# One modulation vector of the second layer is computed in the first FFN instead of at the end of the first mixing

## Chip, cores and metric

The kernel runs on one core of one Trainium2 chip. The metric is the device time of one execution in microseconds. Before the change the median of three runs is 1867.49 us (1861.09, 1867.49 and 1871.28).

## What is computed

Two layers of a diffusion backbone, over 256 context and 256 latent tokens of width 1024, in float32. Cut to what matters here:

```python
for l in range(DEPTH):                     # DEPTH = 2
    sh1, sc1, g1, sh2, sc2, g2 = jnp.split((s_lat @ mod_w[l] + mod_b[l])[:, None, :], 6, axis=-1)
    csh1, csc1, cg1, csh2, csc2, cg2 = jnp.split(s_ctx @ mod_w[l] + mod_b[l], 6, axis=-1)
    ... = _split(modulate(x, sh1, sc1) @ w_in[l], IN_SPLITS)
    ...
    o_l = gated_merge(gt_l, att_l @ w_o_attn[l],
                      short_conv(ch_l, cb_l, cc_l, conv_w[l]) @ w_o_conv[l],
                      rwo_l @ w_o_rwkv[l]) @ w_out[l]
    x_new = layer_norm(alpha * x + g1 * o_l, ln1_g[l], ln1_b[l])
    x_new = layer_norm(alpha * x_new + g2 * swiglu(modulate(x_new, sh2, sc2), ffn_w13[l], ffn_w2[l]),
                       ln2_g[l], ln2_b[l])
```

Each layer has six modulation vectors per stream: shift, scale and gate of the mixing (numbers 0, 1, 2) and of the FFN (3, 4, 5). They depend on the conditioning alone, not on the tokens, so they can be computed at any time before they are used. The pair (l, i) names vector i of layer l; both streams are computed together. (1, 0) is the shift of the second layer's mixing. It is first read at the end of the first layer's FFN, where the second norm's output is modulated for the second layer.

## The kernel before

All 512 tokens go through a layer together. A layer has two parts. The first is the mixing: the input projection in output blocks of 128 (features of the recurrent branch, compressed attention inputs, conv inputs, gates), the chunked scans of the recurrent branch, the attention, and three merges that add the branches, each through its output weights `wo` (function `merge`). Then the output projection, and the second part, the FFN: a loop over 22 turns `m` (line 865), each with two weight tiles of 1024x128 (gate and up, 48 matmuls in all), then a loop over 22 rows of the second weight.

Float32 products are made from three matmuls of split operands: each weight tile is loaded to `raw`, cast by ScalarE to `hi` (line 193), and VectorE or GpSimd makes `lo`, the remainder (line 194). `mm3` (lines 237 to 240) does the three matmuls. `raw` is a ring of three buffers (line 179), and `hi` and `lo` have four halves each.

The modulation vectors are computed in steps. One step (`mod`, line 253) loads 512 KB of `modw` into the same ring of `raw` buffers and does eight small matmuls (line 259). Every second step ends with a copy (line 265), a pick matmul (line 266) and an addition (line 291). A vector is eight steps. After a gate vector (2 or 5) one more step transposes it and stores it by rows (`mod_rows`, line 276).

The table `MODS` says which vectors are made in which list: for each layer, one list for the mixing and one for the FFN. In the first mixing a step follows each of the 24 gate blocks (line 614) and two steps stand in each of the four conv blocks (line 601); `mod_step(100)` on line 619 takes whatever is left of the list. In the first FFN two steps follow the first norm (line 852), one stands in each turn `m` of the loop while `m < N_FFN` (line 885), and line 934 takes the rest at the end.

In the first FFN the kernel also prepares 35 weight tiles of the second layer ahead of time (`ahead_list`, line 217): load `wraw`, cast `whi` on ScalarE (line 230), remainder `wlo` on GpSimd (line 231), and store both (lines 233 and 234).

The order of the program is not the order of the code alone: a scheduler places the instructions of each engine by its own estimate of time and respects data and buffers. All loads and stores named here are issued by SyncE, in order. `brs` are the loaded tiles of a branch, cast to `br` (line 642); `gts` are gate tiles and share three buffers with `brs`.

Of the kernel before, what the change touches and what calls it, by code (L numbers as in the profile page):

```python
# [51 lines left out]
N_CONV = (2, 1)  # L52
BC = 4
X_AT = 0
N_FFN = 10
N_LN1 = (2, 7)
LATE_AT = (2, 4, 6, 8)

# [1 line left out]
CP = 6  # L60
CONV_AT = (20, 4)
WO_EARLY = (2, 0)
MODS = ((((0, 2), (0, 3), (0, 4), (0, 5), (1, 0)), ((1, 1), (1, 2))), (((1, 3), (1, 4)), ((1, 5),)))
FLUSH = (30, 30)
DV = 0
UB = 1
# [10 lines left out]
def body(ctx: ExitStack, tc: tile.TileContext, A: dict, out: bass.AP, dbg=None, upto=None):  # L77
# [203 lines left out]
    def mod_list(todo, bank=None):  # L281
        for l, i in todo:
            for k0 in range(0, 8, MG):
                ps = []
                for j in range(MG):
                    def f(l=l, i=i, k0=k0, j=j, ps=ps):
                        if j == 0:
                            ps.append((bank or pg)())
                        mod(ps[0], l, i, k0 + j, j)
                        if j == MG - 1:  # L290
                            dve.tensor_tensor(out=modT[l][:, i, k0:k0 + MG], in0=mod_out(ps[0], MG),
                                              in1=mod_bias(l, i, k0, MG), op=ALU.add)
                    yield f
            if i in (2, 5):
                yield lambda l=l, i=i: mod_rows(l, i, bank)
# [152 lines left out]
    def layer(l, xh=None, xl=None, pre=()):  # L448
# [6 lines left out]
        share[0] = SHARE[l][0]  # L455
        mods = mod_list(MODS[l][0])

        def mod_step(n=1):
            for _ in range(n):
                f = next(mods, None)  # L460
                if f:
                    f()
# [344 lines left out]
        with ff, tc.tile_pool(name=f"ff{l}", reuse_waits="tile", bufs=1) as fp, banks(f"psf{l}"):  # L807
# [40 lines left out]

            mods = mod_list(MODS[l][1], pg if l else pf)
            one = post(l, 0, accs, fp, x2_out, res1, lambda tt: res_d[0 if l == 0 else 2][tt])  # L850
# [14 lines left out]
            for m in range(KF):  # L865
# [18 lines left out]
                hh.append(hl)  # L884
                if m < N_FFN:
                    mod_step()
# [510 lines left out]
```

## Time and profile before

| | |
|---|---|
| median of three runs | 1867.49 us |
| profiled execution | 1872.44 us |
| its span, first to last instruction | 1870.6 us |
| mean granted TensorE clock | 0.975 |
| TensorE matmuls busy | 1787.7 us, 96% |
| VectorE, ScalarE, GpSimd busy | 58%, 45%, 29% |
| DMA | 379.40 MB, 203 GB/s over the span |

The profile comes from one execution. The granted clock is TensorE's, as a share of its full 2.4 GHz; it has two levels, 2.4 and 1.2 GHz, and a figure between is a mean over a stretch. Busy time of TensorE counts a matmul until its modelled end. In the views an instruction is named by its engine, its line, its output and inputs by the program's names, and "<-" in brackets says what ended the idle time ahead of it. A float32 matmul (the modulation step, a transpose) is counted as two.

### The profile page before, as it was taken

The page shows a single profiled execution, that of the slowest core. Times are in us where ns is not written, and L with a number is a line of the kernel's source. Part 1 is how long each engine was busy: PE and PEld are TensorE (multiplying, and loading weights), DVE is VectorE, ACT ScalarE, POOL GpSimd, SP SyncE. Part 2 cuts the span into 40 slices and gives each one's busy share as a digit, 9 for nine tenths or more (in the row PEclk, how much of TensorE's full clock was granted, in tenths as well). Part 3 has the DMA queues.
Part 4 walks back from the last instruction along what each step waited for, and adds up shares of the span by engine and source line. Part 5 has one row for each costly group of instructions (what it writes and reads, how often), then busy time and mean ns, then how long its engine had stood idle before and what let it go on. Part 6 is the DMA issues. An engine that isn't in the chain of part 4 may idle for free.

```text
span 1870.6 us, 35371 instructions
## 1 busy us (share of the span) xinstructions
PE 1787.7 (96%) x13556; PEld 1469.7 (79%) x13556; DVE 1091.3 (58%) x2012; ACT 842.6 (45%) x1830; POOL 534.2 (29%) x550
## 2 busy tenths in 40 slices
PE   7999999999989999999999999999999999979997
PEld 5777877777768767877888887888788886869986
DVE  4457723873367777643444336168874468866655
ACT  2567333823245442444444313386524364535552
POOL 1466113611134221454343003344311132320001
PEclk9998999999989999999999999998899999989999
DMA  9443544343494326699999424775586673686563
GB/s 341 136 144 108 164 135 158 105 151 124 161 315 158 127 64 235 224 370 350 344 349 348 161 92 156 233 238 171 182 273 221 215 227 112 192 288 223 182 225 110
DMA packets 182410, 379.40 MB, mean 203 GB/s; under 512 B 33952, under 2 KB 89312, under 8 KB 182240
## 3 DMA queue, kind: packets, MB, share of 16 engines
q1 hardware_dynamic: 179264, 368.54, 58.8%
q10 hardware_dynamic: 2976, 8.59, 1.3%
q8 instruction: 107, 1.75, 0.4%
q14 instruction: 63, 0.52, 0.1%
HBM read 301.53 MB, written 75.53 MB: 202 GB/s over the span
## 4 chain that ended last, share of the span: by engine, by line
PE 71%; DMA 10%; DVE 9%; ACT 5%; issue 3%; SPq 1%; POOL 1%; ACTq 0%; POOLq 0%; DVEq 0%
PE pg L238 10%; PE pg L239 10%; PE pg L240 9%; PE p_f L238 9%; PE p_f L240 8%; PE p_f L239 8%; DMA raw<-in_win_dram 3%; PE p_G L1069 2%; PE p_G L755 2%; DVE lo L194 1%; DMA raw<-in_modw_dram 1%; ACT hi L193 1%; PE p_y L776 1%; PE pg L259 1%; DMA raw<-in_w_dram 1%
## 5 line engine op out<-in xcount | busy, mean ns | idle before, releaser
L194 DVE TENSOR_TENSOR lo<-raw,hi 128x512 fp32r<-128x512 f32 (+1 forms) x408 | 321.9, 799 | 352.5 <-ACT hi L193 348.9
L193 ACT CAST hi<-raw 128x512 fp32r<-128x512 f32 x478 | 286.9, 615 | 430.9 <-DMA raw<-in_win_dram 95.1
L238 PE MATMUL pg<-xh,hi 128*128 128x512 f32 (+1 forms) x912 | 331.6, 365 | 8.7 <-ACT gt L585 3.8
L240 PE MATMUL pg<-xh,lo 128*128 128x512 f32 (+1 forms) x912 | 327.0, 359 | 0.7 <-DMA lo<-win 0.6
L239 PE MATMUL pg<-xl,hi 128*128 128x512 f32 (+1 forms) x912 | 326.1, 358 | 0.4 <-DVE xl L246 0.4
L238 PE MATMUL p_f<-x2h,hi 128*128 128x256 f32 (+1 forms) x688 | 232.7, 338 | 4.6 <-ACT hi L193 4.6
L240 PE MATMUL p_f<-x2h,lo 128*128 128x256 f32 (+1 forms) x688 | 231.7, 337 | 0.9 <-DVE lo L194 0.5
L239 PE MATMUL p_f<-x2l,hi 128*128 128x256 f32 (+1 forms) x688 | 231.3, 336 | 0.0
L238 PEld LDWEIGHTS pg<-xh,hi 128*128 128x128 f32 x912 | 177.8, 196 | 40.1 <-issue 9.0
L240 PEld LDWEIGHTS pg<-xh,lo 128*128 128x128 f32 x912 | 178.8, 196 | 26.2 <-issue 3.0
L239 PEld LDWEIGHTS pg<-xl,hi 128*128 128x128 f32 x912 | 178.4, 196 | 22.6 <-issue 1.3
L194 POOL TENSOR_TENSOR lo<-raw,hi 128x512 fp32r<-128x512 f32 x70 | 92.0, 1314 | 342.8 <-ACT hi L193 279.1
L238 PEld LDWEIGHTS p_f<-x2h,hi 128*128 128x128 f32 x688 | 131.4, 191 | 19.7 <-ACT hi L193 6.5
L240 PEld LDWEIGHTS p_f<-x2h,lo 128*128 128x128 f32 x688 | 131.3, 191 | 15.3 <-DVE lo L194 2.1
L239 PEld LDWEIGHTS p_f<-x2l,hi 128*128 128x128 f32 x688 | 131.4, 191 | 12.8
L231 POOL TENSOR_TENSOR wlo<-wraw,whi 128x512 fp32r<-128x512 f32 x70 | 93.5, 1357 | 125.0 <-ACT whi L230 125.0
L334 POOL TENSOR_TENSOR rs<-rs,mhalf 128x1 f32<-128x1 f32 x12 | 8.8, 733 | 359.3 <-DVE rs L353 359.3
L1053 POOL TENSOR_TENSOR FM<-ta,di 64x256 f32<-64x256 f32 x64 | 56.0, 876 | 48.0 <-ACT FM L1047 17.3
L661 POOL TENSOR_TENSOR acc<-acc,gts 128x512 f32<-128x512 f32 (+1 forms) x32 | 38.4, 1209 | 80.0 <-DVE gts L659 61.9
L259 PE MATMUL pg<-raw,cs 128*32 128x128 f32 x1024 | 53.1, 303 | 6.0 <-DMA raw<-in_modw_dram 5.3
L1109 DVE TENSOR_TENSOR sq<-sq,iv 128x31 f32<-128x31 f32 (+15 forms) x124 | 49.2, 397 | 3.2
L483 POOL TENSOR_TENSOR nb<-pp 128x512 f32<-128x512 f32 (+1 forms) x30 | 30.4, 1012 | 71.8 <-ACT pp L480 60.5
(393 smaller groups left out, 3604.3 us busy)
## 6 DMA issues: line engine op xcount, KB each, us to landing
raw<-in_modw_dram SPq DMA_DIRECT2D x96, 512.0 KB, 4.8
raw<-in_w_dram SPq DMA_DIRECT2D x88, 512.0 KB, 5.1
raw<-in_win_dram SPq DMA_DIRECT2D x79, 512.0 KB, 4.4
raw<-in_ffn_w_dram SPq DMA_DIRECT2D x44, 512.0 KB, 3.8
wraw<-in_win_dram SPq DMA_DIRECT2D x35, 512.0 KB, 6.7
win<-whi SPq DMA_DIRECT2D x35, 512.0 KB, 6.0
win<-wlo SPq DMA_DIRECT2D x35, 512.0 KB, 5.4
hi<-win SPq DMA_DIRECT2D x70, 256.0 KB, 3.8
```

The costliest lines, as they stand in the source:

```text
L193: act.copy(out=hi, in_=r)
L194: e.tensor_tensor(out=lo, in0=r, in1=hi.bitcast(F32), op=ALU.subtract)
L231: pool.tensor_tensor(out=lo[:, s], in0=raw[:, s], in1=hi[:, s].bitcast(F32), op=ALU.subtract)
L238: pe.matmul(ps, wh, xh, start=first, stop=False, skip_group_check=True)
L239: pe.matmul(ps, wh, xl, start=False, stop=False, skip_group_check=True)
L240: pe.matmul(ps, wl, xh, start=False, stop=last, skip_group_check=True)
L259: pe.matmul(ps[32 * (k % 4):32 * (k % 4) + 32, 0:128], cs[:, o:o + 32], raw[:, k], start=(j == 0 and k < 4), stop=(k >= 4), skip_group_che ...
L661: pool.tensor_tensor(out=a, in0=a, in1=g, op=ALU.add)
L755: pe.matmul(ps[:, 0:nk], qT[:, h, qt * 128:(qt + 1) * 128], kT[:, h, 0:nk], start=True, stop=True)
L1053: pool.tensor_tensor(out=FM[r, :, k0:k0 + 64], in0=rc(ta[r]), in1=rc(Pi[r]), op=ALU.mult)
L1069: pe.matmul(ps[:, j * 128:j * 128 + ncol], FM[r, j], AR[z][r, e, hp, j, 0:ncol], start=True, stop=True)
L1109: dve.tensor_tensor(out=Ti[:, j + 1:32, 0:w], in0=Ti[:, j + 1:32, 0:w], in1=tv, op=ALU.subtract)
```

## The change

Vector (1, 0) moves from the end of the first mixing's list to the head of the first FFN's list. The steps in the loop of the FFN are allowed in 18 turns instead of 10. The code of the functions is the same.

```diff
-N_FFN = 10
+N_FFN = 18
...
-MODS = ((((0, 2), (0, 3), (0, 4), (0, 5), (1, 0)), ((1, 1), (1, 2))), (((1, 3), (1, 4)), ((1, 5),)))
+MODS = ((((0, 2), (0, 3), (0, 4), (0, 5)), ((1, 0), (1, 1), (1, 2))), (((1, 3), (1, 4)), ((1, 5),)))
```

The first mixing's list goes from 42 steps to 34, of which 32 are taken beside the gates and conv blocks. The first FFN's list goes from 17 steps to 25: 2 after the norm, 10 or 18 in the loop, and 5 at the end either way.

The first place is TensorE at the end of the first mixing, between the transpose of the first layer's last gate vector (line 276) and the merge of the conv branch. `br` numbers are the branch's tiles, `pg` the output blocks. Before:

```order
L276 MATMUL pg<-ident,modT_81 16x128
L259 MATMUL pg<-raw,cs 32x128 x24
L266 MATMUL pg<-pick,modrow 128x4
L259 MATMUL pg<-raw,cs 32x128 x16
L266 MATMUL pg<-pick,modrow 128x4
L1251 MATMUL p_y<-ident,gn 128x128 x4
L259 MATMUL pg<-raw,cs 32x128 x8
L1236 MATMUL p_y<-ident,Yf 128x128 x4
L1270 MATMUL p_G<-sg,lw 128x256
...
L1270 MATMUL p_G<-sg,lw 128x256
L259 MATMUL pg<-raw,cs 32x128 x8
L238 MATMUL pg<-br,hi 128x512
```

With the change:

```order
L276 MATMUL pg_5688<-ident_69,modT0_81 16x128
L238 MATMUL pg_5800<-br_5770,hi_5790 128x512
L238 MATMUL pg_5816<-br_5770,hi_5790 128x512
L238 MATMUL pg_5842<-br_5770,hi_5832 128x512
L239 MATMUL pg_5800<-br_5770,hi_5790 128x512
L240 MATMUL pg_5800<-br_5770,lo_5791 128x512
L238 MATMUL pg_5800<-br_5775,hi_5790 128x512
...
L238 MATMUL pg_5842<-br_5785,hi_5836 128x512
L1251 MATMUL p_y_6190<-ident_69,gn_6182 128x128 x4
```

The 64 matmuls of eight steps are gone from here, and the merge follows the transpose, with three output blocks on the branch's first tile, then the second, to the fourth.

The second place is SyncE at the same time, the loads of the steps (`raw<-in_modw`), of the weights of the merge (`in_wo`) and of the attention (`in_wukv`, `in_wuq`), and of the branch's four tiles (`brs`):

```order
 L586 DMA gate_6_139<-gt 256x1x256
-L256 DMA raw<-in_modw_dram 128x1024
+L180 DMA raw<-in_wo_dram 128x1024
...
-L256 DMA raw<-in_modw_dram 128x1024
+L180 DMA raw<-in_wo_dram 128x1024
 L586 DMA gate_7_140<-gt 256x1x256
-L256 DMA raw<-in_modw_dram 128x1024
-L1226 DMA vv<-feat_13_116 128x256
+L180 DMA raw<-in_wukv_dram 128x1024
 L640 DMA brs<-br_1_0_207 128x512
 L640 DMA brs<-br_1_1_208 128x512
+L640 DMA brs<-br_1_2_209 128x512
...
-L256 DMA raw<-in_modw_dram 128x1024 x3
-L640 DMA brs<-br_1_2_209 128x512
+L180 DMA raw<-in_wuq_dram 128x768
 L640 DMA brs<-br_1_3_210 128x512
```

Where the steps were loaded, weights of the merge and of the attention are loaded now, and the third tile of the branch comes next to the first two.

The third place is ScalarE in the first FFN's loop. A turn runs from one activation `su` to the next; `whi` are the tiles prepared ahead, `hh` the hidden tile, `hi` a weight tile's two halves. The turn that stands once in the program before:

```order
L876 ACTIVATE su<-p_f 128x512
L230 CAST whi<-wraw 128x512 x2
L245 CAST hh<-su 128x512
L193 CAST hi<-raw 128x512 x4
L230 CAST whi<-wraw 128x512 x2
```

With the change, four turns later:

```order
L876 ACTIVATE su<-p_f 128x512
L230 CAST whi<-wraw 128x512 x2
L193 CAST hi<-raw 128x512 x2
L265 COPY modrow<-p_f 128x128
L245 CAST hh<-su 128x512
L193 CAST hi<-raw 128x512 x2
L230 CAST whi<-wraw 128x512 x2
L876 ACTIVATE su<-p_f 128x512
L230 CAST whi<-wraw 128x512 x2
L245 CAST hh<-su 128x512
L193 CAST hi<-raw 128x512 x4
L230 CAST whi<-wraw 128x512 x2
```

The turn with the hidden tile ahead of all four casts comes again after four turns, three times in all.

## Rows read from the trace of the kernel before

**Rows 1.** The chain of waits, whole run, by engine.

```profile
PE 71%; DMA 10%; DVE 9%; ACT 5%; issue 3%; SPq 1%; POOL 1%; ACTq 0%; POOLq 0%; DVEq 0%
```

**Rows 2.** Windows: length, busy PE PEld DVE ACT POOL, clock, DMA share, GB/s.

```profile
530.00:553.50 23.50, 16.86 (x199) 11.39 (x197) 13.24 (x31) 12.20 (x28) 6.46 (x9) 0.71 0.88 304
```

**Rows 3.** Windows, first FFN's loop with steps and without.

```profile
788.90:897.60 108.70, 107.08 (x587) 85.05 (x581) 46.43 (x63) 46.85 (x88) 54.34 (x40) 1.00 0.98 362
897.60:1017.30 119.70, 119.70 (x529) 99.10 (x529) 54.42 (x67) 59.22 (x105) 49.20 (x38) 1.00 0.96 342
```

**Rows 4.** Timeline of TensorE from the transpose to the merge (start, us, instruction).

```profile
536.07 0.28 PE L276 MATMUL pg<-ident,modT 128*16 128x128 f32 x1 [0.20 <-DVE modT L291]
536.27 1.94 PE L259 MATMUL pg<-raw,cs 128*32 128x128 f32 x32
...
544.13 1.09 PE L1251 MATMUL p_y<-ident,gn 128*128 128x128 f32 x4
...
548.29 1.11 PE L1236 MATMUL p_y<-ident,Yf 128*128 128x128 f32 x4 [1.69 <-ACT Yf L1254]
...
551.42 1.22 PE L1270 MATMUL p_G<-sg,lw 128*128 128x256 f32 x2
...
553.47 0.50 PE L238 MATMUL pg<-br,hi 128*128 128x512 f32 x1
```

**Rows 5.** Timelines of SyncE and ScalarE, the branch's tiles.

```profile
534.69 1.11 SPq L640 DMA_DIRECT2D brs<-br  x2
...
539.33 1.32 ACT L245 CAST br<-brs 128x512 fp32r<-128x512 f32 x2 [0.65 <-DMA brs<-br]
...
546.21 0.62 ACT L245 CAST br<-brs 128x512 fp32r<-128x512 f32 x1 [3.61 <-DMA brs<-br]
```

**Rows 6.** Windows, after a wait of TensorE that ends at 734.

```profile
732.00:740.00 8.00, 6.00 (x24) 5.19 (x25) 7.59 (x18) 2.87 (x6) 1.27 (x2) 0.79 0.77 295
```

**Rows 7.** Windows, late in the first attention.

```profile
676.00:680.00 4.00, 4.00 (x29) 2.40 (x27) 3.14 (x12) 1.57 (x7) 0.00 (x0) 1.00 0.00 0
```

**Rows 8.** Timeline of VectorE, line 877, one per turn of the loop.

```profile
788.86 0.69 DVE L877 TENSOR_TENSOR su<-su,p_f 128x512 f32<-128x512 f32 x1 [0.94 <-PE p_f L240]
...
859.99 0.69 DVE L877 TENSOR_TENSOR su<-su,p_f 128x512 f32<-128x512 f32 x1 [9.72 <-PE p_f L240]
872.17 0.69 DVE L877 TENSOR_TENSOR su<-su,p_f 128x512 f32<-128x512 f32 x1 [7.32 <-PE p_f L240]
885.65 0.69 DVE L877 TENSOR_TENSOR su<-su,p_f 128x512 f32<-128x512 f32 x1 [2.50 <-PE p_f L240]
897.61 0.69 DVE L877 TENSOR_TENSOR su<-su,p_f 128x512 f32<-128x512 f32 x1 [1.60 <-PE p_f L240]
...
1017.29 0.69 DVE L877 TENSOR_TENSOR su<-su,p_f 128x512 f32<-128x512 f32 x1 [1.55 <-PE p_f L240]
```

**Rows 9.** Timelines of ScalarE and TensorE, the turn that ends at 885.65.

```profile
872.89 0.62 ACT L245 CAST hh<-su 128x512 fp32r<-128x512 f32 x1 [4.20 <-DVE su L877]
873.41 2.18 ACT L193 CAST hi<-raw 128x512 fp32r<-128x512 f32 x4
...
874.08 0.50 PE L238 MATMUL p_f<-x2h,hi 128*128 128x512 f32 x1 [1.45 <-ACT hi L193]
```

**Rows 10.** Waits of SyncE's queue, 795 to 1030 (us in total, times, longest).

```profile
SPq L180 <- PE p_f L259: 11.6, 5, 3.2
```

**Rows 11.** DMA issues in the loop with steps (count, KB, us to landing).

```profile
raw<-in_w_dram SPq DMA_DIRECT2D x20, 512.0 KB, 6.2
```

**Rows 12.** Windows, one turn's length of the loop.

```profile
828.80:840.50 11.70, 11.70 (x65) 9.29 (x64) 3.97 (x6) 4.69 (x9) 3.87 (x4) 1.00 1.02 408
```

**Rows 13.** Windows, second layer's mixing, scans and attention.

```profile
1180.00:1637.00 457.00, 439.27 (x4220) 375.24 (x4220) 299.22 (x598) 231.66 (x558) 139.07 (x166) 0.96 0.65 205
```

## The prediction

> **What bounds the kernel now.** I read the chain of waits first, for what ends the run: 71% of it is TensorE, 10% DMA and 9% VectorE [rows 1]. So time is won where TensorE waits, and an operation put where it is dense is paid in full. Next I read busy time by stretch, for the place the vector's steps leave and the place they go to. The place they leave, from 530.0 to 553.5 us, is one of the thinnest of the run: 16.86 of 23.5 us busy, at a mean granted clock of 0.71 [rows 2]. The place they go to is full: in the first FFN's gate-and-up loop TensorE is busy 107.08 of 108.7 us while steps run beside it, and 119.7 of 119.7 us after they have stopped, with the DMA engines at 0.98 and 0.96 [rows 3]. The change moves work from a loose stretch to a tight one, so the sum is a difference of two like numbers.
>
> A "step" below is one call of the modulation list: a 512 KB load and eight small matmuls, which the profile counts as 16. Eight steps make one vector; every second one adds the small pick matmul.
>
> **What leaves the end of the first mixing.** The program order of TensorE (first excerpt) shows eight steps gone from between the transpose of line 276 and the first matmul of the conv branch's merge. In the timeline that transpose starts at 536.07 and the merge at 553.47 [rows 4]. In between stand those eight steps, from 536.27 on, and four groups that stay: L1251 (1.09 us), L1236 (1.11) and L1270 twice, the longer 1.22.
>
> When could the merge start without the steps? It needs the branch's first tile. Its load is issued at 534.69, and ScalarE casts the first tile at 539.33, two tiles in 1.32 us, so the first is ready 0.66 us later, at about 540.0 [rows 5]. The merge's weights are no longer last: the SyncE order (second excerpt) gives their loads the freed buffers, ahead of the branch's tiles. So the merge starts at 540.0 instead of 553.47: **13.5 us earlier**. Two things are given back:
> - The four groups that stay move into dense work. Here they take at most 1.09 + 1.11 + 1.22 + 1.22 = 4.6 us at near the half clock; at the full clock half of it, 2.3 us.
> - TensorE idles before 540 and comes back at the lower of its levels. The nearest row is the return after the wait that ends at 734: in 732 to 740 the mean granted clock is 0.79, a loss of 0.21 x 8 = 1.7 us [rows 6].
>
> That leaves 13.5 - 2.3 - 1.7 = **9.5 us won**. The bounds: at best nothing is given back, 13.5 us. At worst the merge waits for its fourth tile. That shares three buffers with the first three; here the third is cast at 546.21, 0.62 us [rows 5], and a merge from 546.8 wins 553.5 - 546.8 - 4.0 = 2.7 us. I take 9.5 because the new order runs tile by tile over three output blocks: nine matmuls on each of the first three tiles, 27 in all, enough to reach the fourth.
>
> **What is moved with it at no charge.** By the same order of TensorE all 96 matmuls of the conv branch's merge now come ahead of the attention, where 48 did before, so the attention has 48 fewer to fill its waits. I cost this at nothing: late in the attention, where almost no merge matmul is left, TensorE is still busy 4.00 of 4.00 us and VectorE 3.14 [rows 7]. If that cover fails, 48 matmuls of 0.227 us (10.88 us of a loop turn over its 48, below) stand idle: 10.9 us.
>
> **What comes to the first FFN.** The su rows of VectorE mark the turns of the loop. With a step in each, six turns take 859.99 - 788.86 = 71.13 us, 11.86 each; without, eleven take 1017.29 - 897.61 = 119.68, 10.88 each [rows 8]. A step costs 0.98 us of dense TensorE, so eight cost **7.8 us**.
>
> The two turns after those six are worse: 12.18 and 13.48 us, 1.95 us over [rows 8]. The reason stands on ScalarE. There the cast of the hidden tile (872.89), which waits for the end of the turn's matmuls, comes ahead of the casts of both weight tiles of the next turn (873.41), and TensorE waits 1.45 us for them [rows 9]. This is the order in which the program issues, not chance. Before the change the pattern (activation, two ahead casts, hidden tile, four weight casts) occurs once; in the changed program three times (third excerpt), because the steps' loads go on. Two more cost 2 x 1.95 = **3.9 us**. The bounds are 0, if the weights' casts turn out to be covered, and 3.9. I take 3.9, since the same rows on the same engine come in the same order.
>
> On SyncE the moved loads stand ahead of weight loads. A weight load already waits five times, 11.6 us in all, for a buffer that a step's matmuls hold [rows 10]; eight more loads may bring as many again. I charge them nothing beyond the two casts, because a weight load lands in 6.2 us [rows 11] and a turn is 10.9 us or more.
>
> **Sum.** -9.5 + 7.8 + 3.9 = +2.2 us. The five last steps (the gate vector's) stay after the FFN in both. The profiled execution took 1872.4 us (span 1870.6 and 1.8 around it) and would take 1874.6; the median of the three runs is 1867.5, 4.9 below it, so I forecast **1869.7 us**. The three runs lie 10 us apart, so 0.5% (9.3 us) is about what can be told from no change.
>
> **Rivals.**
> *The DMA engines have no room (slower).* Eight loads of 0.524 MB are 4.19 MB; at the loop's 342 GB/s [rows 3] that is 12.3 us. If the weight loads come late by that, TensorE waits it out and the 3.9 us are in it: -9.5 + 7.8 + 12.3 = +10.6, 1878.1 us. It decides from the point where waiting on SyncE and landing together exceed one turn. For it: shares of 0.96 and 0.98, and the waits on SyncE [rows 10]. Against it: much of that traffic is weights for layer 2 that can slip past the loop, and one turn-long stretch moved 408 GB/s with TensorE full [rows 12]. The Trainium skill ("DMA: Bandwidth & Descriptors", Specifications) puts the limit of a core's HBM traffic at about 358 GB/s; by that rule the loop is full and 4.19 MB cost an estimated 11.7 us. The trace agrees only with the mean: its 408 GB/s goes above it. Chance 0.15.
>
> *The gap gives all and the FFN takes little (still no change).* -13.5 + 7.8 = -5.7, 1861.8 us. For it: the four small groups may fit between the merge's first matmuls. Against it: it needs no stall at a pattern that stalled once already. Chance 0.10.
>
> *Another order further on (either side).* The scheduler reorders all that follows, also the second layer's mixing and scans, though the work is the same. From 1180 to 1637 TensorE idles 457.0 - 439.3 = 17.7 us and the clock of 0.96 loses some 18 more [rows 13]. If a third of these 36 us goes or comes: 12 us, 1857.7 with the forecast's other terms, or 1881.7. Nothing in the profile says which; the idle pieces are many and short. With it goes the attention's lost cover (10.9 us), which is only a loss. Chance 0.09 faster, 0.06 slower.
>
> That the change doesn't do what it says is ruled out by the order of the program.
>
> **The numbers.** Forecast 0.60; rivals 0.15, 0.10, 0.09 and 0.06. Over 0.5% faster (below 1858.2) holds the 0.09 and 0.03 of the second rival's edge: 0.12. Slower (above 1876.8) holds 0.15 and 0.06: 0.21. The rest, 0.67, is no change. The range runs from the faster case, 1858, to the slower one, 1881, and leaves out about 0.1; the forecast alone spans 1866 to 1877, from the bounds of the gap (-13.5 + 11.7 and -2.7 + 11.7).
>
> **What would show it.** In the profile after: no step between the transpose of line 276 and the merge, and the merge 11 to 14 us earlier; 18 turns of the FFN loop at 11.9 us and four at 10.9, three of them 1.5 us longer with an idle of TensorE that the cast of a weight tile ends; the attention about as long as before. Wrong would be: a merge that starts at 546 or later; turns past the tenth over 12.5 us that DMA ends; or stretches after 1180 that differ by more than 5 us while the first layer comes out as said.

## The result, and the profile after

The changed kernel takes 1889.36 us (median of 12 runs, 1872.72 to 1903.44) where the kernel before takes 1867.22 in the same session (12 runs): a ratio of 1.0111, with a 95% interval of 1.0091 to 1.0131. The ratio leaves out the longest of the 12 executions, which is over 1.5% above the fastest. The change makes the kernel slower by some 20 us. The forecast was 1869.7 us, and its range ended at 1881.

The profile after comes from the fastest of those 12 runs: 1872.72 us, span 1870.9, against 1872.44 and 1870.6 in the profile before. Laid side by side, these two show no loss at all. The reading of one trace against another is therefore checked below with six more traces of the changed kernel and one more of the kernel before.

The chain of waits by engine, to be held against [rows 1]:

```profile
PE 71%; DVE 10%; DMA 9%; ACT 5%; issue 4%; POOL 1%; SPq 1%; ACTq 0%; POOLq 0%; DVEq 0%
```

Nothing has changed hands; what happened is found stage by stage. The windows that answer to [rows 2], to the loop of [rows 3] (its two halves, steps in both) and to [rows 13]; columns as there:

```profile
530.00:553.50 23.50, 21.64 (x85) 16.83 (x86) 16.25 (x31) 10.29 (x22) 5.65 (x5) 0.80 0.72 230
771.00:898.00 127.00, 125.29 (x679) 99.33 (x678) 55.72 (x66) 53.78 (x100) 66.38 (x47) 1.00 0.96 355
898.00:1022.20 124.20, 120.88 (x605) 95.97 (x604) 49.34 (x72) 53.75 (x100) 45.41 (x34) 0.97 0.94 338
1180.00:1637.00 457.00, 434.94 (x4231) 373.18 (x4230) 296.60 (x597) 230.49 (x557) 141.18 (x169) 0.97 0.66 206
```

The loose stretch is filled: 21.64 of 23.5 us instead of 16.86. The first half of the loop idles 1.7 us, about as before (1.6). The second half, without any idle before, now idles 3.3 us and runs at 0.97 of the clock.

The timeline of TensorE from the transpose to the merge, to be held against [rows 4]:

```profile
533.34 0.38 PE L276 MATMUL pg<-ident,modT 128*16 128x128 f32 x1 [0.82 <-DVE modT L291]
534.63 1.65 PE L238 MATMUL pg<-br,hi 128*128 128x512 f32 x3 [0.92 <-ACT br L245]
536.08 0.63 PE L239 MATMUL pg<-br,hi 128*128 128x512 f32 x1
...
539.45 0.40 PE L238 MATMUL pg<-br,hi 128*128 128x512 f32 x1
```

The merge starts 1.29 us after the transpose; before, it was 17.40. Counted from the transpose that is 16.1 us earlier, more than the 13.5 forecast. The branch's loads are no longer between loads of steps. The timelines of SyncE and ScalarE, for [rows 5]:

```profile
528.74 1.40 SPq L640 DMA_DIRECT2D brs<-br  x3
...
533.97 1.36 ACT L245 CAST br<-brs 128x512 fp32r<-128x512 f32 x2
```

Three tiles are issued together at 528.74 (two at 534.69 before). The turns of the first FFN's loop, line 877 on VectorE, for [rows 8]:

```profile
768.39 0.69 DVE L877 TENSOR_TENSOR su<-su,pg 128x512 f32<-128x512 f32 x1 [0.51 <-ACT su L876]
...
861.48 0.69 DVE L877 TENSOR_TENSOR su<-su,p_f 128x512 f32<-128x512 f32 x1 [7.32 <-PE p_f L240]
875.03 0.69 DVE L877 TENSOR_TENSOR su<-su,p_f 128x512 f32<-128x512 f32 x1 [9.07 <-PE p_f L240]
...
911.17 0.69 DVE L877 TENSOR_TENSOR su<-su,p_f 128x512 f32<-128x512 f32 x1 [8.45 <-PE p_f L240]
926.33 0.69 DVE L877 TENSOR_TENSOR su<-su,p_f 128x512 f32<-128x512 f32 x1 [10.68 <-PE p_f L240]
...
962.48 0.69 DVE L877 TENSOR_TENSOR su<-su,p_f 128x512 f32<-128x512 f32 x1 [7.34 <-PE p_f L240]
977.57 0.69 DVE L877 TENSOR_TENSOR su<-su,p_f 128x512 f32<-128x512 f32 x1 [2.55 <-PE p_f L240]
989.54 0.69 DVE L877 TENSOR_TENSOR su<-su,p_f 128x512 f32<-128x512 f32 x1 [1.60 <-PE p_f L240]
1000.42 0.69 DVE L877 TENSOR_TENSOR su<-su,p_f 128x512 f32<-128x512 f32 x1 [1.56 <-PE p_f L240]
...
1022.18 0.69 DVE L877 TENSOR_TENSOR su<-su,p_f 128x512 f32<-128x512 f32 x1 [0.81 <-PE p_f L240]
```

From the first to the last su row the loop takes 253.8 us; before it took 238.2. There are three long turns, as forecast. The first (875.03 - 861.48 = 13.55) is the one that was there before (13.48). The two new ones are longer, 15.16 and 15.09. ScalarE and TensorE in the first of these, for [rows 9]:

```profile
911.90 0.62 ACT L245 CAST hh<-su 128x512 fp32r<-128x512 f32 x1 [2.90 <-DVE su L877]
912.42 2.18 ACT L193 CAST hi<-raw 128x512 fp32r<-128x512 f32 x4
```

```profile
913.09 0.50 PE L238 MATMUL p_f<-x2h,hi 128*128 128x512 f32 x1 [1.45 <-ACT hi L193]
...
916.25 0.63 PE L238 MATMUL p_f<-x2h,hi 128*128 128x512 f32 x1
916.67 0.63 PE L239 MATMUL p_f<-x2l,hi 128*128 128x512 f32 x1
...
918.33 0.39 PE L238 MATMUL p_f<-x2h,hi 128*128 128x512 f32 x1
```

The hidden tile's cast again stands ahead of all four weight casts, and TensorE again idles 1.45 us for them. But then matmuls follow each other at 0.43 us instead of 0.227. The windows of these microseconds show why (the column ahead of the last two is the granted clock):

```profile
914.00:916.00 2.00, 2.00 (x7) 1.59 (x8) 1.65 (x3) 1.74 (x4) 0.49 (x1) 0.71 0.91 354
916.00:918.00 2.00, 2.00 (x7) 1.52 (x6) 0.00 (x0) 0.00 (x0) 2.00 (x2) 0.50 1.03 422
918.00:920.00 2.00, 2.00 (x10) 1.66 (x9) 0.00 (x0) 0.00 (x0) 0.02 (x1) 0.94 1.09 412
```

The clock falls to 1.2 GHz and the loss is (0.29 + 0.50 + 0.06) x 2 = 1.7 us, on top of the stall. The same happens in the third long turn. The waits of SyncE's queue for a buffer that a step's matmuls hold, over the loop from its first to its last su row (us in total, times, longest; line 256 loads the steps, line 180 the weights):

```profile
SPq L256 <- PE p_f L259: 40.8, 8, 7.9
SPq L180 <- PE p_f L259: 14.6, 7, 3.2
```

Over the same stretch of the kernel before, the steps' loads wait 7.0 us in two waits, and the weights' loads 13.2 in six ([rows 10] begins later and shows five of them). So the weights' loads wait hardly longer than before, as the prediction assumed; it is the steps' own loads that now wait for the ring.

### Stage by stage, over several traces

The marks are the transpose of line 276 in [rows 4], the first and the last su row (line 877), the first sums of norms in the second layer (line 948) and the end of the span. "Layer 1" here runs from the transpose to line 948, "layer 2" from there to the end. The column "to first su" is called the gap below, and the gap's gain is what the change takes off it. The traces come from several chips; in the five sessions that timed it more than once, the kernel before has medians of 1866.5 to 1868.8 us, so the chips differ little. All in us:

| traces | transpose at | to first su | loop | to line 948 | layer 1 | layer 2 | span |
|---|---|---|---|---|---|---|---|
| before, [rows 4, 8] and rest of that trace | 536.1 | 243.0 | 238.2 | 150.2 | 631.4 | 703.1 | 1870.6 |
| before, second trace | 531.3 | 243.1 | 238.2 | 149.6 | 630.9 | 696.0 | 1858.2 |
| changed, mean of seven | 536.2 | 234.9 | 252.7 | 150.1 | 637.7 | 708.6 | 1882.4 |
| changed, lowest and highest | 531.3, 540.3 | 233.0, 237.1 | 250.5, 255.3 | 149.3, 152.2 | 634.3, 640.2 | 698.9, 715.1 | 1870.9, 1890.8 |
| difference of the means | +2.4 | -8.2 | +14.4 | +0.2 | +6.5 | +9.0 | +18.0 |

Up to the transpose TensorE, VectorE and ScalarE do the same in the same order, and the place of the transpose varies by 9 us among the seven traces, so +2.4 is taken as scatter. The first layer loses 6.5 us on the mean, and 3 to 9 in every single trace. The second loses 9.0 on the mean, but from -1 to +16 in single traces, and there are only two traces of the kernel before to hold them against. Both together are 15.5 of the 18.0 us of the spans, which are close to the 20 of the medians.

### The profile page after: what moved, and what is told of

Read it like the earlier page. It is cut to its first block, busy times and chain, and to the rows that moved or that the text cites. A ratio compares the mean times of both kernels' runs of the same rounds, so it can differ in the third digit from the quotient of the medians.

```text
span 1870.9 us, 35353 instructions
## 1 busy us (share of the span) xinstructions
PE 1783.4 (95%) x13556; PEld 1466.3 (78%) x13556; DVE 1081.2 (58%) x2012; ACT 839.3 (45%) x1830; POOL 536.3 (29%) x550
## 4 chain that ended last, share of the span: by engine, by line
PE 71%; DVE 10%; DMA 9%; ACT 5%; issue 4%; POOL 1%; SPq 1%; ACTq 0%; POOLq 0%; DVEq 0%
PE pg L238 10%; PE pg L239 9%; PE p_f L240 9%; PE pg L240 9%; PE p_f L238 9%; PE p_f L239 9%; DMA raw<-in_win_dram 3%; PE p_G L1069 2%; DVE lo L194 1%; PE p_G L755 1%; PE pg L259 1%; PE p_y L776 1%; DMA raw<-in_w_dram 1%; ACT hi L193 1%; PE p_c L1191 1%
## 5 line engine op out<-in xcount | busy, mean ns | idle before, releaser
L194 DVE TENSOR_TENSOR lo<-raw,hi 128x512 fp32r<-128x512 f32 (+1 forms) x408 | 317.2, 791 | 305.3 <-ACT hi L193 302.1
L877 DVE TENSOR_TENSOR su<-su,p_f 128x256 f32<-128x256 f32 (+1 forms) x43 | 23.7, 551 | 90.4 <-PE p_f L240 89.3
L1069 PE MATMUL p_G<-AR,FM 64*128 64x128 f32 x384 | 51.9, 293 | 0.9 <-ACT tms L1083 0.8
```

The source lines that it names most:

```text
L194: e.tensor_tensor(out=lo, in0=r, in1=hi.bitcast(F32), op=ALU.subtract)
L877: dve.tensor_tensor(out=su[:, q0:T], in0=su[:, q0:T], in1=pw[1][:, q0:T], op=ALU.mult)
L1069: pe.matmul(ps[:, j * 128:j * 128 + ncol], FM[r, j], AR[z][r, e, hp, j, 0:ncol], start=True, stop=True)
```

## The experiments

Two theories came first. **A**: the loss is in the first FFN's loop, in the stalls and the clock behind them. **B**: the second layer, which the scheduler orders anew (970 of TensorE's 4550 rows there stand in another place), loses by its new order.

**The changed kernel once more** (no edit).

> The changed kernel once more, for a second profile: the median of its 12 runs (1889.4 us) lies 16.6 us above the execution that was profiled, and the slower runs show a lower mean clock (0.963 to 0.973 against 0.975). Theory A (the first FFN's loop): the three turns that cast all four weight halves behind the hidden tile stall TensorE, its clock falls after them, and a typical run shows a loop (first to last su) over 253.8 us, the profiled one's, with a clock under 0.97 there. Theory B (further on): the loop takes 253 to 255 us again, and the extra time stands after 1180 us, in the reordered second layer.

Measured: 1884.14 us, clock 0.968. The loop took 252.1 us, less than in the first trace, so theory A's loop over 253.8 is not there. Layer 1 took 636.5 us and layer 2 708.2. Of the 11.4 us over the first trace's span 9.3 are in layer 2.

**The vector left out.**

```diff
+    pool.memset(modT[1][:, 0], 0.0)
-MODS = ((((0, 2), (0, 3), (0, 4), (0, 5), (1, 0)), ((1, 1), (1, 2))), ...
+MODS = ((((0, 2), (0, 3), (0, 4), (0, 5)), ((1, 1), (1, 2))), ...
```

> The vector (1, 0) is not computed at all (it is set to zero), so only the first part of the change is made: the eight steps leave the first mixing and come nowhere else. Theory A: the gap's gain alone, 8 to 10 us, 1857 to 1860 us, with the spread of the kernel before. Theory B: the order of the second layer differs as it does with the change, and costs as there: 1875 us or more, with a lower clock.

Measured: 1876.0 us, ratio 1.0044 (1.0021 to 1.0066): slower, though it does less, as B expected. The trace has layer 1 at 622.5 us, 8.6 shorter than before, exactly the gap's gain, and layer 2 at 715.3. Theory A alone is out: some 17 us are lost outside layer 1.

**The vector made twice**, in the mixing as before and again in the FFN.

```diff
-N_FFN = 10
+N_FFN = 18
-MODS = ((((0, 2), (0, 3), (0, 4), (0, 5), (1, 0)), ((1, 1), (1, 2))), ...
+MODS = ((((0, 2), (0, 3), (0, 4), (0, 5), (1, 0)), ((1, 0), (1, 1), (1, 2))), ...
```

> The vector is made in the first mixing as before and once more in the first FFN, 18 turns of it with a step: only the second part of the change, and eight steps more work. Theory A: the eight steps (8 us), three stalls and the clock behind them, 1885 to 1900 us, with the changed kernel's spread of runs. Theory B: eight steps and little else, 1874 to 1879 us.

Measured: 1877.59 us, 1.0056 (1.0036 to 1.0076). The loop took 254.8 us, so it alone costs 16.6, without the gap's gain. Six of its turns have the hidden tile ahead of all four casts; they take 13.45 to 13.64 us, and the clock did not fall in any of them. Layer 2 took 690.3 us, less than in any other trace. So the total is what B expected (1874 to 1879), but not for B's reason: the loop cost twice the eight steps, and layer 2 gave much of it back.

**The vector's steps in the conv blocks**, four in each, instead of at the end.

```diff
-N_CONV = (2, 1)
+N_CONV = (4, 1)
```

> The list as before the change, but four steps instead of two in each of the four conv blocks of the first mixing, so that two steps instead of ten are left at its end; the first FFN is as before. Theory A: the gap's gain (8 to 10 us) pays for eight steps among dense matmuls (8 us): 1865 to 1869 us. Theory B: a reordered second layer again, 1875 us or more.

Measured: 1885.4 us, 1.0088 (1.0064 to 1.0112). The FFN's loop is untouched (238.5), and layer 2 took 712.6 us. But line 948 comes at 1174.6 us, where the two traces of the kernel before have it at 1167.5 and 1162.2, so 7 to 12 us are lost ahead of layer 2, all of it before the FFN's loop, and this run says little of the order. In single traces, three other orders of layer 2 gave 690 to 715 us, against 696 and 703 in the kernel before.

**Crossing the two.** With two steps fewer in the loop, the scheduler's order of layer 2 flips. The changed kernel with 16 steps has the old order of layer 2, row for row; the kernel before with 8 has the new one.

```diff
-N_FFN = 18
+N_FFN = 16
```

> The changed kernel with 16 steps allowed in the first FFN's loop instead of 18; two more of the list are taken at the end of that FFN. The vector is made in the first FFN, as in the change. In the program, every engine's order in the whole second layer is then row for row that of the kernel before (the change has some 970 of TensorE's 4550 rows there in another place). Theory A (the loss is the steps in the first FFN's loop, their stalls and the clock behind them): nearly all the steps are still there, one stall of three may go, so 1881 to 1888 us. Theory B (the loss is the second layer's other order): the first layer keeps up to +6 us of the changed kernel's and the second layer takes what it takes before, so 1862 to 1874 us, and from the second layer's first norm sums to the end as long as before within 5 us.

Measured: 1875.56 us, 1.0059 (1.0030 to 1.0088).

```diff
-N_FFN = 10
+N_FFN = 8
```

> The kernel before with 8 steps allowed in the first FFN's loop instead of 10; two more are taken at the end of that FFN. The vector stays at the end of the first mixing. In the program, every engine's order in the second layer is then row for row that of the changed kernel. Theory A: two steps of 0.98 us leave the loop and come back behind it, so no change, 1863 to 1871 us. Theory B: the first layer as before, the second as long as in the changed kernel, so 1877 to 1888 us, with a granted clock below that of the kernel before.

Measured: 1868.48 us, 1.0017 (0.9993 to 1.0042). The first lies between what A and B expected, the second is A's (no change). So neither theory holds alone. With the old order the version with 16 steps still costs 11 us, of which 7 stand behind the loop, where the changed kernel loses nothing; the new order alone costs 3, perhaps nothing. The trace with 16 steps has layer 1 at 642.3 us (+11.2: loop 248.3, and 157.0 behind the loop, where seven steps are left instead of five) and layer 2 at 699.2, as before. The trace with 8 has 631.4 and 700.9.

**A third order**: the kernel before with `N_FFN = 12`.

> The kernel before with 12 steps allowed in the first FFN's loop instead of 10; two fewer are left for its end. The second layer gets a third order (some 1050 of TensorE's 4550 rows in another place than before, in other places than in the change too). Theory A: two more steps and at most one more stall in the loop, two steps less behind it: 1866 to 1872 us. Theory B: the order the kernel had before is a lucky one, like the three other orders tried, this one costs 5 to 20 us: 1872 to 1887 us.

Measured: 1872.47 us, 1.0038 (1.0014 to 1.0061), layer 1 631.3, layer 2 714.6. With layer 1 as long as before, this order costs some 7 us.

**The kernel before once more.**

> The kernel before once more, for a second trace of it: the executions of one program differ by some 10 us, so a stage's length has to be seen twice before a difference of a few microseconds in it is read. Both theories: 1858 to 1876 us. The first layer up to the second layer's first norm sums within 2 us of the first trace; what scatter there is, B expects behind that point, in the granted clock.

Measured: 1860.01 us. Layer 1 is within 0.5 us of the first trace; the scatter lies ahead of it and behind it.

**Taking the stalls away.** Theory **C**: the stalls come from the ring of three buffers that steps and weights share. **D**: they come from DMA without room. The steps of the first FFN get one buffer of their own.

```diff
-    cnt, share = [0], [3]
+    cnt, share, steps = [0], [3], [None]
...
-        raw = (pl or ring).tile([128, 8, 128], F32, tag="raw", name="raw", bufs=8 if pl else 3)
+        raw = (pl or steps[0] or ring).tile([128, 8, 128], F32, tag="raw", name="raw", bufs=8 if pl else 1 if steps[0] else 3)
...
-            mods = mod_list(MODS[l][1], pg if l else pf)
+            mods, steps[0] = mod_list(MODS[l][1], pg if l else pf), fp if l == 0 else None
```

> The changed kernel, but the steps in the first FFN load their 512 KB to a buffer of their own instead of the ring of three that the FFN's weights use. In the program ScalarE then has, in every turn of the loop, at least two of the next weights' casts ahead of the hidden tile's cast (in the changed kernel all four stand behind it in five turns, in the kernel before in two). Theory C (the loss in the first layer is those turns' stalls of TensorE and the clock behind them, made by the shared ring): the loop takes its 238.2 us of before plus 8 steps of 0.98, 244 to 247 us, and no turn is over 12.5 us. Theory D (the loss there is the DMA queues, 95% busy with 512 KB more in eight turns): the loop stays at 250 us or more. The whole time under C: 5 to 9 us below the changed kernel by the loop, the second layer has another order again and adds -8 to +10, so 1865 to 1885 us; under D 1880 to 1895.

(The counts of turns there should read three and one, as in the third excerpt.) Measured: 1889.37 us, 1.0114 (1.0082 to 1.0146), no gain as a whole; by windows, the loop's halves and the stretch behind it:

```profile
775.00:897.00 122.00, 122.00 (x668) 97.17 (x667) 55.58 (x69) 55.04 (x100) 59.97 (x45) 1.00 0.98 362
897.00:1019.00 122.00, 122.00 (x630) 98.36 (x629) 51.57 (x70) 57.07 (x103) 46.74 (x36) 1.00 0.97 356
1019.10:1183.90 164.80, 152.19 (x766) 126.73 (x765) 67.87 (x115) 43.53 (x80) 18.15 (x23) 0.96 0.42 142
```

The loop is what C expected: 245.5 us with 18 steps, TensorE never idle, although the DMA engines are at 0.97. D is out, though the total lies where D had put it and not where C had. The reason is that 14.6 us are lost behind the loop, by a flaw of the edit: the last five steps share the one buffer too, and wait for each other's loads. Two such waits are 7.6 us of it (us in all, times, longest):

```profile
PE p_f L259 <- DMA raw<-in_modw_dram: 7.6, 2, 7.1
```

**The same with 16 steps**, so with seven left.

> As the run with the steps' own buffer, with 16 steps allowed in the loop. The second layer's order is then that of the kernel before with 12 steps (two of TensorE's rows apart), so against that run (1.0038 of the kernel before) only the first layer differs: the place of the vector, without the ring's stalls. Theory C: the steps are only moved, the gap of the first mixing gives back what the loop takes, so 1.001 to 1.006, 1868 to 1878 us; against the 16 steps in the shared ring (1.0059) 3 to 10 us less. Theory D: as the 16 steps in the shared ring or slower, 1.0055 to 1.012.

Measured: 1903.0 us, 1.0176 (1.0147 to 1.0205). Loop 243.6, without idle; behind it 173.7 us, 24 more than before. C's total (1868 to 1878) was missed, most of it by that.

**The changed kernel, timed again and traced again.**

> The changed kernel, timed again on the chip of these runs. Its first traces add up to some 7 us in the first layer, and the two pairs of kernels with the same second layer to some 7 us for the second layer's order, so theory C expects a ratio of 1.005 to 1.010, near the lower end of the first measurement (1.0091 to 1.0131). If it is 1.010 or more, some 7 us are lost in a place that the traces so far don't show. The trace: first layer from the transpose to the second layer's first norm sums 636 to 640 us (631 before).

> One more trace of the changed kernel, to see where its slower executions lose the clock. Theory C: the loop of the first FFN 252 to 254 us as in the first two traces, so what differs from trace to trace lies elsewhere, above all between 1200 and 1360 us, where the two traces so far have 15 and 22 us of clock loss (15 and 12 in the two of the kernel before). Theory D: the loop itself varies with the DMA, by 3 us or more.

Measured: 1884.22 us, 1.0096 (1.0061 to 1.0130), and 1880.62. Layer 1 took 640.2 and 637.1, the loop 253.6 and 252.1, as C expected. Theory C's sum was near its upper end, so layer 2 had to cost more than the first two traces showed.

**The own buffer up to the end of the loop alone.** The edit above, and, so that the last steps load to the ring again:

```diff
-            lat = tts if last else [2, 3, 0, 1]
+            lat, steps[0] = tts if last else [2, 3, 0, 1], None
```

With `N_FFN = 16` (old order of layer 2) and 18 (the third order), and beside them the changed kernel with `N_FFN = 20` and the ring (the third order too). Theory **E**: layer 2 scatters whatever its order.

> The changed kernel with 16 steps allowed in the first FFN's loop, and with a buffer of their own for the steps in the loop alone (the steps behind the loop load to the ring again). The second layer's order is that of the kernel before (8 of the last 4400 TensorE rows apart). Theory C: stretch from the transpose to the loop 8 us shorter than before, loop 243 to 245 us (238.2 before, 248.3 with 16 steps and the ring), the end of the FFN with 7 steps left 7 us longer (157, as in both runs with 7 steps), the second layer as before: +4.6 us in all, a ratio of 1.000 to 1.005, below the 1.0059 of the same kernel with the ring. Theory E (the second layer's length scatters whatever its order, so that the order explains nothing): 1.006 or more is as likely as less, and the second layer is off the three traces of this order (696 to 703 us from its first norm sums to the end) by 8 us or more.

> The same with 18 steps allowed, as in the change, and 5 left for the end as before. The second layer's order is that of the kernel before with 12 steps (1.0038). Theory C: transpose to loop 8 us shorter than before, loop 245 to 247, end of the FFN 150: the first layer as long as in the kernel before within 2 us, and the second as long as with 12 steps: 1.001 to 1.006. Theory E: the second layer apart from that of the run with 12 steps (714 us) by 8 us or more.

> The changed kernel with 20 steps allowed in the loop, through the ring, and 3 left for the end. The second layer's order is exactly that of the kernel before with 12 steps and of the run before this one. ScalarE's order in the loop has again three turns with all four casts behind the hidden tile's. Theory C: loop 254 to 258 us (253 with 18 steps, 0.98 for each of two more), so 7 to 10 us above the run with the own buffer: a ratio of 1.006 to 1.011. Theory E: no step between the two runs, within 0.003 of each other.

Measured: 1.0041 (1.0013 to 1.0069), 1.0034 (1.0009 to 1.0058) and 1.0080 (1.0050 to 1.0111). All three ratios are where C put them, though not all of their parts, as said below the windows. The loops of the three traces by windows, the 18 and 16 steps with the own buffer first, then the 20 through the ring:

```profile
775.90:1021.40 245.50, 245.50 (x1315) 196.65 (x1304) 108.20 (x142) 113.85 (x205) 107.59 (x81) 1.00 0.97 358
```

```profile
772.00:1015.50 243.50, 243.50 (x1281) 195.77 (x1270) 105.97 (x140) 113.34 (x204) 108.45 (x81) 1.00 0.97 357
```

```profile
775.20:1027.50 252.30, 246.28 (x1323) 194.78 (x1322) 105.72 (x139) 109.23 (x205) 117.94 (x84) 1.00 0.97 355
```

With 18 steps and their own buffer, layer 1 is 634.2 us, 3.0 over the kernel before, and 149.4 of it lie behind the loop, as before. What misses C's sum is the gap: it is 239.3 and 238.3 us long, so it gives 3.7 and 4.7 us where C counted on 8. The two steps ahead of the loop share the one buffer as well, and in the trace with 18 steps TensorE waits 1.6 us for their load there and 2.4 for a cast that cost 0.6 in the changed kernel. The ring costs the third kernel 6.0 us of idle. Its layer 1 (637.9) is only 3.7 longer than that of the kernel with 18 steps and the own buffer, so more than half of the 8.6 us between their ratios lies outside layer 1, and that C's 7 to 10 came out is luck in part. Its loop of 252.3 is under the 254 to 258 expected: the clock did not fall in it. In the third order, layer 2 took 702.8, 708.7, 714.6 and 717.1 in four traces; E is right in so far that one order scatters by as much as two orders differ (702.8 is 12 us from the first trace of that order), so a single trace of layer 2 decides nothing and the medians must.

**Where the slower executions lose.** Three more traces of the changed kernel; theory **F** put their loss into the first FFN.

> The changed kernel once more, for the traces of its slower executions: four traces have spans of 1871 to 1882 us, the timed ones reach 1902 with a mean granted clock of 0.963. Theory C: the first layer from the transpose to the second layer's first norm sums 636 to 640 us again, whatever the whole time is; an execution slower than 1885 is so behind that point, between 1200 and 1400 us, by more and longer falls of the clock than the 15 to 27 us of clock loss there in the traces so far. Theory F (the slow executions lose it in the first FFN): loop over 257 us.

> As the run before this one: first layer 636 to 640 us from the transpose; what an execution is slower lies between 1200 and 1400 us by theory C, in the loop by theory F.

> As the two runs before this one: first layer 636 to 640 us from the transpose; what an execution is slower lies between 1200 and 1400 us by theory C, in the loop by theory F.

Measured: 1890.26, 1892.57 and 1885.99 us. Layer 1 is 637.7, 639.3 and 634.3, layer 2 713.5, 715.1 and 713.0. F is out: the loops are 255.4, 251.2 and 250.5 us. The first part of layer 2, from line 948 to the long triangular products of the scans (line 1191, `LBa`), by windows: first the kernel before (both traces), then the changed one (its first trace and its slowest).

```profile
1167.50:1358.60 191.10, 184.21 (x1280) 153.47 (x1278) 116.92 (x225) 114.83 (x304) 76.90 (x101) 0.92 0.67 206
```

```profile
1162.20:1351.20 189.00, 181.37 (x1279) 150.51 (x1277) 116.09 (x225) 114.62 (x304) 77.60 (x101) 0.94 0.67 208
```

```profile
1172.00:1360.60 188.60, 178.19 (x1253) 148.53 (x1251) 115.40 (x227) 115.48 (x306) 74.23 (x101) 0.92 0.66 199
```

```profile
1175.70:1379.30 203.60, 193.03 (x1254) 162.73 (x1252) 116.74 (x228) 115.76 (x306) 74.31 (x101) 0.84 0.59 184
...
1348.00:1382.00 34.00, 32.12 (x400) 28.74 (x400) 13.71 (x21) 13.83 (x31) 5.77 (x8) 0.55 0.42 133
```

The work is the same within a few per cent of the matmuls, but the clock is at 0.84 in the slowest: the stretch loses 0.16 x 203.6 = 33 us of clock there, against 15 (0.08 x 191.1) in the kernel before. Not all of that is time, since the stretch is only 12.5 us longer. At its worst the clock is at 0.55 for 34 us, where TensorE is called busy 32 of 34. Over the seven traces this stretch is 194.2 us long, 4.2 over the kernel before's 190.0; the other 4.8 of the 9.0 lie behind it, in pieces of 1 to 5 us. So C is half right: the slowest of the three loses in this stretch, against the first trace, but 1885.99 is 5.3 us longer in it (193.9) and 8.8 behind it.

## Why the prediction was wrong

**The gap: right in the sum, by luck in part.** Forecast 9.5 us won, measured 8.2 (from the transpose to the first su row). Both of its parts were off, and the two errors cancel in part. The merge came 16.1 us earlier instead of 13.5, because I kept the issue time of the branch's loads at 534.69 although the steps' loads ahead of them were gone. And 7.9 us were given back instead of 4.0: besides the four small groups, TensorE waits longer in the stretch behind the merge, where I had costed the moved work at nothing. From the first attention scores to the first su row TensorE idles 173.0 - 162.1 = 10.9 us, where it idled 7.0. The kernel before by windows, then the changed one:

```profile
594.10:779.10 185.00, 178.00 (x987) 136.38 (x986) 139.76 (x301) 79.47 (x186) 44.98 (x35) 0.98 0.43 145
```

```profile
595.40:768.40 173.00, 162.12 (x921) 123.65 (x921) 130.70 (x288) 72.07 (x173) 39.73 (x30) 0.98 0.42 142
```

Two waits make most of the difference: one for VectorE's norm (`zt`, line 414) is 4.7 us instead of 2.3, and one for a branch's cast tiles (`br`), 1.2 us, is new. All seven traces of the changed kernel have both (3.7 to 5.4 us and 1.1 to 1.7). That the 48 matmuls fewer are what lengthens them is not shown.

**The steps in the loop: right.** 0.98 us each was forecast; with the stalls taken away, the loop takes 243.6 us with 16 and 245.5 with 18, 0.95 each.

**The stalls: mechanism right, size wrong.** Two more turns with the hidden tile ahead of all four casts came, where and as forecast, and went with the shared ring. The term was 3.9 us and measured 14.4 - 7.8 = 6.6. I took the price of a stall from the one turn of the kernel before, in which the clock held. In the two new ones it fell in 9 of 14 cases over the seven traces, for 1.7 us each, as the lengths of the turns show (15.1 to 15.2 us with a fall, 13.5 to 13.6 without).

**DMA without room: rightly not taken.** The loop ran at 358 GB/s over 245.5 us with no idle of TensorE at all. The rule of the Trainium skill ("DMA: Bandwidth & Descriptors", Specifications) of about 358 GB/s agrees with that mean; an estimated 11.7 us of waiting did not follow from it, since the loads kept up.

**Nothing further on: the step that failed.** The sum put the second layer's other order at 0, and its rival at 12 us either way with a chance of 0.06 for slower. Measured are +9.0 us in the traces, and 11 to 14 if layer 1's 6.5 is taken off what the two ratios say. That is at least half of the loss, and with the stalls' 2.7 over the forecast it carries the result past the range. I had seen the size of what lay there (18 us of idle and 18 of clock in [rows 13]) and that the order changes, and still took the forecast's 0 as the likely case. Stretches after 1180 us that differ while the first layer is near the forecast are one of the signs of being wrong that the prediction had named.

How much of it is the order? Not all, and why the rest came is open. The changed kernel with the old order of layer 2 is at 1.0059 and 1.0041, and its first layers (+11.2 and +6.4 us, by the traces) explain these without the second: 0 and 1 us are left. For the third order 3 to 11 us are left over four kernels, and with the vector left out 17, in an order of its own. For the new order with the changed first layer 11 to 14 are left, but the kernel before with that same new order is at 1.0017, and about 3 are left (the interval takes in 0). So the same order of layer 2 came with two costs, and what joins it to the first layer was not found. These differences rest on a trace or two each, beside the medians.

The clock is at most a part of it. Over the first part of layer 2 the changed kernel's traces lose 15 to 33 us of clock, and those of the kernel before 12 and 15. But the kernel before with 8 steps loses 27 us there, and its stretch is no longer (190.7 us; columns as above):

```profile
1164.20:1354.90 190.70, 181.71 (x1227) 153.07 (x1225) 114.12 (x227) 113.20 (x303) 74.14 (x100) 0.86 0.62 189
```

Its 12 executions have a mean granted clock of 0.970, like the changed kernel's (0.968 and 0.970; 0.974 to 0.975 for the kernel before), and yet its time is 1.0017. Which idle of TensorE makes the clock fall there was not isolated; that stays open.

**No version beat the kernel before.** The best with the vector in the FFN is the one with its own buffer in the loop and 18 steps, at 1.0034. By the sum of separate traces the move itself is close to a draw: the gap gives 8.2 us, and eight steps of dense TensorE take 7.6 to 7.8. No run shows both at once: where the stalls are gone, the gap gave only 3.7 to 4.7.

## What to carry to other kernels

Moving work out of a thin stretch pays only what that stretch gives at the next mark behind it, and costs full price where it goes; here both were some 8 us. A load that enters a ring of buffers shared with the main loop can reorder an in-order engine's queue: count in the program how often the awaited operation comes ahead of all the prefetches, and price each case with the fall of the clock behind it, not with the stall alone. Where a scheduler orders the rest of the program anew, don't take that as free: give it the scatter seen in that part as its range, on both sides, and compare several traces, since the fastest execution of the slower kernel looked like the kernel before.

## What the runs showed of the hardware that was not expected

The same stall of TensorE, 1.45 us, left the clock at its upper level in one turn (13.55 us) and was followed by 1.2 GHz in the next long one (15.16 us), in one execution. The longer executions of the changed kernel mostly have the lower mean granted clock: from a span of 1870.9 us at 0.975 to 1900.1 at 0.962, which is 47 and 72 us of lost clock for 29 us of span. But between programs the mean clock doesn't tell which is slower: 0.970 went with a ratio of 1.0017 in the kernel before with 8 steps, and with 1.0096 in the changed one. And TensorE can be called busy 94% of 34 us (32.12 us) while the clock stays at 0.55 of full speed.
